# A third second-level product in the second block's second map, with weight sums and residual work placed elsewhere

## The chip, the cores and the metric

The kernel runs on one core of a Trainium2 chip. The metric is device time in microseconds (us) of one execution. A core has a matrix engine (TensorE, in profiles PE, with its weight loads PEld), three other engines that compute (VectorE or DVE, ScalarE or ACT, GpSimd or POOL) and a sync engine (SyncE or SP); each takes its instructions in order. SP issues most loads and POOL most stores. Data lie in SBUF, 128 partitions wide; TensorE's results go to eight PSUM banks.

## What is computed

One decoder layer over 2048 tokens of width 1024: a token mixer (convolution and pooling groups, one output projection), then a squared-ReLU MLP of hidden width 4096, each followed by a scaled residual and a layer norm. Cut to what matters here:

```python
h = x * (1.0 + sc2) + sh2
f = jnp.square(jax.nn.relu(h @ w_mlp_in[l])) @ w_mlp_out[l]
x = _layer_norm(DEEPNORM_ALPHA * x + (1.0 + g2) * f, ln2_g[l], ln2_b[l])
```

The first product of the MLP is called its first map below, the second its second map.

## The kernel before

The tokens go through in two blocks of 1024, b = 0 and b = 1, each through the input projection, the output projection, the first map (`up`, eight groups g) and the second map (`down`). Every product is made at higher precision from two halves: ScalarE rounds a tile to its high part (L81), VectorE makes the low part (L82), and `mm3` issues three matmuls (L86 to L88). A large product is done with seven block products instead of eight (Strassen's scheme), on sums of blocks that VectorE forms beforehand and that are stored to memory and loaded again where they are needed: `usum` for the MLP's inner activations, `w2sum` for its second weights.

In `down`, the block products are called coarse: product i is done in two steps (hf 0 and 1), each of 96 matmuls 128x512, into four banks X or Y. The results are combined into the eight tiles `F`. Where b = 1, two of the seven coarse products, i = 1 and i = 5, are done by the same scheme once more, over quarter blocks: seven `fine_*` products m of 48 matmuls 128x256 each (L1094 to L1148, the matmuls at L1120), on sums of quarter blocks of activations (`uquart`) and weights (`wquart`). `FINE` names the products with a fine form and where their operands lie; `save_quarters` makes the activations' sums in `up`, and `sum_blocks` the weights' from `in_w2q` (loads on SP, adds on VectorE, stores on POOL); `QUARTER_SUMS` says how many groups of the weights' sums follow each group g of block 1's first map. The first coarse result (i = 0, "11") is kept in `F`'s second half by `third_row` and added to other results by the rule of the scheme.

Tiles come from rings, named by a letter with a number of buffers: `h` 28, `r`, `w` 6, `o` 12. A tile that is asked for must wait until the tile that had its buffer before has been read for the last time. A scheduler orders each engine's instructions by its own estimate of times, so code that is written in one place can be issued earlier or later, and what decides is the order on each engine and the waits for buffers. The residual of the second layer norm (`residual()`, the tiles `rsave` made from `nsave` with two rows of the norm's parameters) is made beside `down`. The layer norm of the output projection ends in transposes on TensorE (L757).

## Time and profile before

| | |
|---|---|
| median of 3 runs | 1732.28 us (1731.45 to 1732.68) |
| profiled execution | 1732.22 us, its span 1730.2 us, granted clock 0.999 |
| TensorE | 7998 matmuls and transposes in the span |
| fine products (L1120) | 672 matmuls from 1467 to 1548 us |
| loads and stores | 480.48 MB, 278 GB/s on the mean |

The span is what lies between the first and the last instruction; the execution's time is 2 us longer. In block 0 the output projection ends at about 260 us, the first map at about 575, the second map at about 860; in block 1 the first map runs from about 1130 to 1420 and the second to the end. A timeline row has the start, the duration, the engine, the line, the operation with what it writes and reads, and in brackets the idle time ahead of it with what ended it. A windows row has the stretch, then PE, PEld, DVE, ACT and POOL busy in it with their instructions, the clock, the DMAs' busy share and GB/s.

### The profile page before, as it was taken

The numbers are of one execution on the slowest core, as the hardware profiler recorded it, in microseconds if no ns is written. First come the engines' busy times: TensorE is split into PE (matmuls) and PEld (weight loads), VectorE is DVE, ScalarE is ACT, GpSimd is POOL, SyncE is SP. The second block draws the span as 40 slices with busy tenths as digits, with TensorE's granted clock in tenths as the row PEclk, the third lists the DMA queues.
The fourth block names the chain that finished last, engine by engine and source line by source line (L and its number), as shares of the span: only waits on it lengthen the run. The fifth ranks groups of instructions, "written<-read, shape, count | busy, mean of one in ns | idle before, by whom it ended". The sixth has DMA issues, their size and how long they took to land.

```text
span 1730.2 us, 22371 instructions
## 1 busy us (share of the span) xinstructions
PE 1721.4 (99%) x7998; PEld 1440.3 (83%) x7998; DVE 1350.0 (78%) x1762; ACT 879.3 (51%) x1188; POOL 249.0 (14%) x449
## 2 busy tenths in 40 slices
PE   9999999999999999999999999999999999999998
PEld 8888888888888888888888888888888888998886
DVE  8898798877777676769686789688677768987796
ACT  5323358554454655446573344775445555773451
POOL 0222221122322000000000000103222222000020
PEclk9999999999999999999999999999999999999999
DMA  9899868778888998887672366557655589998871
GB/s 386 337 323 354 329 225 283 277 275 317 328 321 324 363 415 329 307 280 268 204 265 76 120 227 211 209 198 260 246 219 201 213 315 399 418 366 301 305 264 52
DMA packets 149647, 480.48 MB, mean 278 GB/s; under 512 B 17680, under 2 KB 18464, under 8 KB 149536
## 3 DMA queue, kind: packets, MB, share of 16 engines
q1 hardware_dynamic: 102528, 313.87, 50.0%
q0 software_dynamic: 47008, 165.19, 25.0%
q8 instruction: 62, 1.02, 0.2%
q14 instruction: 49, 0.40, 0.1%
HBM read 329.56 MB, written 149.43 MB: 277 GB/s over the span
## 4 chain that ended last, share of the span: by engine, by line
PE 99%; DVE 0%; ACT 0%; DVEq 0%; issue 0%
PE ps L87 30%; PE ps L88 30%; PE ps L86 30%; PE ps L1120 5%; PE ps L406 3%; PE ps L757 1%; PE ps L120 0%; PE ps L142 0%; DVE o L1354 0%; DVE o L1348 0%; DVE st L1321 0%; DVE o L91 0%; DVEq L1481 0%; ACT mv L721 0%; ACT mv L722 0%
## 5 line engine op out<-in xcount | busy, mean ns | idle before, releaser
L87 PE MATMUL ps<-h,w 128*128 128x512 f32 x1312 | 510.3, 389 | 0.0
L88 PE MATMUL ps<-h,w 128*128 128x512 f32 x1312 | 510.2, 389 | 0.0
L86 PE MATMUL ps<-h,w 128*128 128x512 f32 x1312 | 510.1, 389 | 0.0
L86 PE MATMUL ps<-h,h 128*128 128x512 f32 (+1 forms) x1000 | 387.7, 388 | 0.0
L88 PE MATMUL ps<-h,h 128*128 128x512 f32 (+1 forms) x1000 | 387.7, 388 | 0.0
L87 PE MATMUL ps<-h,h 128*128 128x512 f32 (+1 forms) x1000 | 387.5, 387 | 0.0
L81 ACT CAST h<-r 128x1024 fp32r<-128x1024 f32 (+1 forms) x196 | 199.2, 1020 | 280.3 <-PE ps L87 152.8
L81 ACT CAST w<-r 128x1024 fp32r<-128x1024 f32 x156 | 164.2, 1053 | 256.7 <-PE ps L87 247.2
L82 DVE TENSOR_TENSOR h<-r,h 128x1024 fp32r<-128x1024 f32 (+1 forms) x196 | 231.4, 1185 | 79.7 <-ACT h L81 79.3
L87 PEld LDWEIGHTS ps<-h,w 128*128 128x128 f32 x1312 | 246.3, 188 | 51.7 <-DVE h L82 0.5
L86 PEld LDWEIGHTS ps<-h,w 128*128 128x128 f32 x1312 | 246.0, 188 | 51.6 <-ACT h L81 0.3
L88 PEld LDWEIGHTS ps<-h,w 128*128 128x128 f32 x1312 | 246.3, 188 | 51.2 <-DVE w L82 0.3
L82 DVE TENSOR_TENSOR w<-r,w 128x1024 fp32r<-128x1024 f32 x156 | 190.5, 1221 | 98.3 <-ACT w L81 97.4
L86 PEld LDWEIGHTS ps<-h,h 128*128 128x128 f32 x1000 | 187.8, 188 | 38.4
L87 PEld LDWEIGHTS ps<-h,h 128*128 128x128 f32 x1000 | 187.8, 188 | 38.2
L88 PEld LDWEIGHTS ps<-h,h 128*128 128x128 f32 x1000 | 187.8, 188 | 38.2
L91 DVE TENSOR_TENSOR o<-o,o 128x1024 f32<-128x1024 f32 (+2 forms) x218 | 186.0, 859 | 43.0 <-DMA usum<-o 36.8
L82 DVE TENSOR_TENSOR h<-w,h 128x1024 fp32r<-128x1024 f32 x124 | 152.3, 1228 | 5.4 <-ACT h L81 5.4
L91 DVE TENSOR_TENSOR o<-o,ps 128x512 f32<-128x512 f32 (+1 forms) x172 | 112.4, 664 | 45.1 <-PE ps L88 44.7
L81 ACT CAST h<-w 128x1024 fp32r<-128x1024 f32 x124 | 130.2, 1050 | 14.8 <-POOL w L1059 4.3
L1003 POOL DMA_DIRECT2D usum<-o x96 | 51.5, 537 | 432.6 <-ACT o L997 199.8
L91 DVE TENSOR_TENSOR r<-r,r 128x1024 f32<-128x1024 f32 x60 | 73.4, 1223 | 14.2 <-DMA r<-in_w 8.7
(153 smaller groups left out, 1439.9 us busy)
## 6 DMA issues: line engine op xcount, KB each, us to landing
usum<-o POOLq DMA_DIRECT2D x96, 512.0 KB, 4.3
r<-usum SPq DMA_DIRECT2D x96, 512.0 KB, 5.2
w<-w2sum SPq DMA_DIRECT2D x64, 512.0 KB, 6.0
r<-in_w SPq DMA_DIRECT2D x60, 512.0 KB, 6.1
o<-in_w SPq DMA_DIRECT2D x72, 256.0 KB, 6.1
w2sum<-o POOLq DMA_DIRECT2D x64, 256.0 KB, 5.9
w<-in_w SPq DMA_DIRECT2D x32, 512.0 KB, 5.8
r<-uquart SPq DMA_DIRECT2D x28, 512.0 KB, 9.7
```

The source lines that it names most:

```text
L81: high = nc.scalar.copy(hi, src)
L82: return high.ins, nc.vector.tensor_tensor(lo, src, hi.bitcast(F32), op=ALU.subtract).ins
L86: nc.tensor.matmul(ps, whi, xhi, start=first, stop=False, skip_group_check=goes_on)
L87: nc.tensor.matmul(ps, whi, xlo, start=False, stop=False, skip_group_check=goes_on)
L88: nc.tensor.matmul(ps, wlo, xhi, start=False, stop=last, skip_group_check=goes_on)
L91: return nc.vector.tensor_tensor(out_, a, b_, op=op)
L406: nc.tensor.matmul(ps[m, h], wt[:, w : w + P], A[k][p // 2][:, hs], start=k == 0 and p == 0, stop=k == KD - 1 and p == 2)
L757: nc.tensor.transpose(ps[:, t * P : t * P + P], R[4 * h + t][:, k * P : k * P + P], ident)
L1003: nc.gpsimd.dma_start(usum[g, i], r)
L1120: nc.tensor.matmul(ps, a[:, us], w[:, gs], start=not begun, stop=hf == 1 and g == 3 and a is ul, skip_group_check=True)
```

## The change

Product i = 0 gets the fine form too: in block 1 the coarse list loses its two steps, and 21 fine products run in place of 14. Its result is made in `F[4..7]`'s first half and copied by ScalarE to the second; the results of k = 1 and k = 5 are then added from there by VectorE, eight adds of 128x512. The activations' quarter sums for it are made in `up` directly for g of 2 and more, and for g = 0 and 1 from a stored copy that is loaded again at g = 3 and 4.

The sums of quarter blocks of weights are twelve groups instead of eight: four are written in block 0's `down`, four in block 1's input projection and four in block 1's `up`. The first eight use a new ring `c` of two buffers, which result 11 of `up` also has, with the gate's vectors `G2` in block 0's `down`; ring `o` has 10 buffers instead of 12. The residual of block 1 is made in two parts: tiles 0 to 3 in `up` at g = 1, 3, 5 and 6 (two loads of rows and one of `nsave`, two VectorE operations, a store), tiles 4 to 7 in `down` by `rest_late`.

The order of the instructions changes well beyond these places. Three of them follow. First TensorE in block 1's first map, where `h_1519`, `h_1522` and their low parts `h_1520`, `h_1523` of before are the operands of one product, which is `h_1538` to `h_1542` after. Before:

```order
L86 MATMUL ps_1451_9094<-h_1519_9470,w_1526_9490 128x512
L86 MATMUL ps_1474_9218<-h_1503_9374,w_1532_9541 128x512
L87 MATMUL ps_1474_9218<-h_1504_9375,w_1532_9541 128x512
L88 MATMUL ps_1474_9218<-h_1503_9374,w_1533_9542 128x512
L86 MATMUL ps_1474_9218<-h_1503_9374,w_1532_9541 128x512
L87 MATMUL ps_1451_9094<-h_1520_9471,w_1526_9490 128x512
L88 MATMUL ps_1451_9094<-h_1519_9470,w_1527_9491 128x512
```

After:

```order
L89 MATMUL ps_1467_9206<-h_1538_9588,w_1545_9608 128x512
L90 MATMUL ps_1467_9206<-h_1539_9589,w_1545_9608 128x512
L89 MATMUL ps_1468_9219<-h_1538_9588,w_1545_9608 128x512
L90 MATMUL ps_1468_9219<-h_1539_9589,w_1545_9608 128x512
L91 MATMUL ps_1467_9206<-h_1538_9588,w_1546_9609 128x512
L89 MATMUL ps_1467_9206<-h_1538_9588,w_1545_9608 128x512
```

Before, matmuls of another product (bank `ps_1474`) stand between those of this one, which begins in its second bank only after six of its own in the first; after, the product runs without a break and goes to its second bank (`ps_1468`) with its third matmul.

On VectorE at the same place, the operations ahead of the low part of the product's last operand (`h_1523` before, `h_1542` after), with the low part of its weights `w_1527` before and `w_1546` after. Before:

```order
L91 TENSOR_TENSOR o_1518_9467<-o_1518_9467,o_1459_9160 128x1024
L91 TENSOR_TENSOR o_1510_9413<-o_1510_9413,ps_1501_9357 128x512
L91 TENSOR_TENSOR o_1502_9370<-o_1502_9370,ps_1451_9094 128x512
L82 TENSOR_TENSOR h_1520_9471<-o_1518_9467,h_1519_9470 128x1024
L91 TENSOR_TENSOR o_1502_9370<-o_1502_9370,ps_1452_9107 128x512
L91 TENSOR_TENSOR o_1521_9474<-o_1521_9474,o_1465_9186 128x1024
L82 TENSOR_TENSOR w_1537_9575<-r_1535_9572,w_1536_9574 128x1024
L82 TENSOR_TENSOR h_1523_9478<-o_1521_9474,h_1522_9477 128x1024
```

After:

```order
L94 TENSOR_TENSOR o_1537_9585<-o_1537_9585,o_1475_9272 128x1024
L94 TENSOR_TENSOR o_1529_9531<-o_1529_9531,ps_1520_9475 128x512
L94 TENSOR_TENSOR o_1521_9488<-o_1521_9488,ps_1467_9206 128x512
L85 TENSOR_TENSOR h_1539_9589<-o_1537_9585,h_1538_9588 128x1024
L94 TENSOR_TENSOR o_1540_9592<-o_1540_9592,o_1481_9298 128x1024
L94 TENSOR_TENSOR o_1521_9488<-o_1521_9488,ps_1468_9219 128x512
L85 TENSOR_TENSOR w_1546_9609<-r_1544_9606,w_1545_9608 128x1024
L85 TENSOR_TENSOR h_1542_9596<-o_1540_9592,h_1541_9595 128x1024
```

The add that empties the second bank (`ps_1452` before, `ps_1468` after) has moved behind a wide add, and the low part of this product's own weights has moved here from well ahead, while the next product's (`w_1537` before) has gone behind it.

On VectorE in block 0's second map, just ahead of the add that empties the first bank of a closing step (`ps_935` before, `ps_937` after). Before:

```order
L82 TENSOR_TENSOR h_1000_6354<-r_997_6349,h_999_6353 128x1024
L82 TENSOR_TENSOR h_1002_6358<-w_998_6351,h_1001_6357 128x1024
L82 TENSOR_TENSOR h_1006_6366<-r_1003_6361,h_1005_6365 128x1024
L82 TENSOR_TENSOR h_1008_6370<-w_1004_6363,h_1007_6369 128x1024
L91 TENSOR_TENSOR o_703_4831<-o_703_4831,ps_935_5925 128x512
```

After, from the third of these on:

```order
L85 TENSOR_TENSOR h_1010_6394<-r_1007_6389,h_1009_6393 128x1024
L85 TENSOR_TENSOR h_1012_6398<-w_1008_6391,h_1011_6397 128x1024
L94 TENSOR_TENSOR c_1259_7951<-c_1259_7951 128x512
L94 TENSOR_TENSOR c_1259_7951<-c_1259_7951,c_1260_7952 128x512
L94 TENSOR_TENSOR c_1260_7952<-c_1259_7951,c_1260_7952 128x512
L94 TENSOR_TENSOR c_1260_7952<-c_1260_7952 128x512
L94 TENSOR_TENSOR o_703_4831<-o_703_4831,ps_937_5939 128x512
```

Four adds of a group of quarter sums stand ahead of the bank's add, and four of another group (`c_1235`, `c_1236`) ahead of the two splits that are left out. On SP the loads of these groups stand among those of the residual and of the operands:

```order
L1082 DMA r_1013_6401<-usum_149 128x1024
L217 DMA w_1021_6444<-in_rows 128x1024
L954 DMA c_1235_7754<-in_w2q 128x512
L1227 DMA r_1019_6438<-rsave_152 128x1024
L217 DMA w_1022_6446<-in_rows 128x1024
L954 DMA c_1235_7754<-in_w2q 128x512
L954 DMA c_1236_7755<-in_w2q 128x512 x2
L1227 DMA r_1026_6487<-rsave_152 128x1024
L1084 DMA w_1042_6605<-w2sum_148 128x1024
L954 DMA c_1259_7951<-in_w2q 128x512
```

Before, the same stretch of SP has the rows without a `c` tile alone. The tile `c_1259` has the buffer that `c_1235` had.

The diff, cut to its core:

```diff
-QUARTER_SUMS = (0, 1, 1, 1, 1, 1, 1, 2)
+QUARTER_SUMS = (0, 0, 1, 0, 1, 1, 0, 1)
...
-        return mk(big, [P, w], dt, "o", 12)
+        return mk(big, [P, w], dt, "o", 10)
+
+    def t_c(w=T):
+        return mk(big, [P, w], F32, "c", 2)
...
             if not last:
+                quarter_sums(t_c)
                 next(groups[j])
+                quarter_sums(t_c)
...
-    FINE = {1: 0, 5: 1}
+    FINE = {0: 2, 1: 0, 5: 1}
+    QUARTERED = {1: 0, 7: 1, 0: 2}
+    REST = {1: 0, 3: 1, 5: 2, 6: 3}
...
+    def rest_of(t, r, ag, ab):
+        nc.vector.scalar_tensor_tensor(r, r, ALPHA, ag, op0=ALU.mult, op1=ALU.mult)
+        nc.vector.scalar_tensor_tensor(r, ab, ALPHA, r, op0=ALU.mult, op1=ALU.add)
+        nc.gpsimd.dma_start(rsave[t], r)
+
+    quarters = [(n, hf, p) for n in (2, 0, 1) for hf in range(2) for p in halves]
+
+    def quarter_sums(tiles):
+        n, hf, p = quarters.pop(0)
+        sum_blocks([w2q[n, i, hf] for i in range(4)], wquart[n, hf], tiles, [p])
...
         product(0, X, True)
-        c11 = keep(X)
+        c11 = keep(X, t_c)
         product(1, Y, True)
         join(c11, Y)
         save(c11, 0)
+        loaded = rest_loads()
...
+        if loaded:
+            rest_of(REST[g], *loaded)
         product(4, X, False)
...
-        coarse = (0, 2, 3, 4, 6) if b else (0, 1, 2, 3, 5, 4, 6)
+        coarse = (2, 3, 4, 6) if b else (0, 1, 2, 3, 5, 4, 6)
...
+            if b == 0 and n in (6, 8, 10, 12):
+                quarter_sums(lambda w: t_c(w))
...
-                    if m == 6:
-                        for t in range(4):
-                            add(t, lo_, X[t])
+                    if part_ < 6:
+                        continue
+                    for t in range(4):
+                        if k == 0:
+                            nc.scalar.copy(F[t + 4][:, hi_], F[t + 4][:, lo_])
+                            continue
+                        cs = lo_ if k == 1 else hi_
+                        tt(F[t][:, cs], F[t][:, cs], F[t + 4][:, lo_], ALU.add)
+                        if k == 5:
+                            add(t, hi_, X[t])
...
+            if b and g in (3, 4):
+                c11 = t_o()
+                nc.sync.dma_start(c11, usum[g - 3, 0])
+                save_quarters(c11, QUARTERED[0], g - 3)
+            for _ in range(QUARTER_SUMS[g] if b else 0):
+                quarter_sums(t_o)
```

More of the change, by code (lines that the diff above doesn't have):

```diff
@@ L1066, in down_operands, with rest_late @@
         return out_, done
+    def rest_late():
+        ag, ab = row(t_c(D), rows[0]), row(t_c(D), rows[1])
+        for t in range(4, 8):
+            yield
+            r = t_r()
+            nc.sync.dma_start(r, nsave[t])
+            rest_of(t, r, ag, ab)
     def residual():
@@ L1125, in quarter_of @@
             c = (H if i == 5 else 0) + col * Q
-            return [F[2 * row + t][:, c : c + Q] for t in range(2)]
+            return [F[(0 if i else 4) + 2 * row + t][:, c : c + Q] for t in range(2)]
         def fine_copy(i, row, col, bank):
@@ L1250, in down @@
         ready = operands(0)
-        later = residual()
+        later = rest_late() if b else residual()
         todo = [(k, m) for k in FINE for m in range(7)]
@@ L1402, in mlp @@
                     sums += [(sum_weights, wins[0], winsum, p) for p in halves]
-        else:
-            sums = [(sum_blocks, [w2q[n, i, hf] for i in range(4)], wquart[n, hf], p)
-                    for n in range(2) for hf in range(2) for p in halves]
         for g in range(NC):
@@ L1409, in mlp @@
                 pass
-            some = (QUARTER_SUMS if b else HALF_SUMS)[g]
-            for make, src, dst, p in sums[:some]:
+            if b and g in (3, 4):
[4 more added lines that the diff above has]
+                quarter_sums(t_o)
+            for make, src, dst, p in sums[:HALF_SUMS[g]]:
                 make(src, dst, t_o, which=[p])
-            del sums[:some]
+            del sums[:HALF_SUMS[g]]
         F = []
```

42 lines of the change are left out of this document (26 added, 16 removed).

## The prediction

> **What bounds the kernel now.** I read the page's busy shares first, then its chain of waits, because with five engines at 14 to 99% only the chain says which of them sets the end.
>
> ```profile
> PE 1721.4 (99%) x7998; PEld 1440.3 (83%) x7998; DVE 1350.0 (78%) x1762; ACT 879.3 (51%) x1188; POOL 249.0 (14%) x449
> ...
> PE 99%; DVE 0%; ACT 0%; DVEq 0%; issue 0%
> ```
>
> TensorE is busy for 1721.4 of 1730.2 us and is 99% of the chain; no other engine holds as much as 1%. There is nothing to win by waiting less: the 9 us left are the load at the head and the last tile's normalisation. So time falls only when TensorE's matmuls cost less, and it rises wherever an operand comes late. The change does a little of the first and moves a great deal of work that feeds TensorE, so the next views are the price of the two kinds of matmul and the stages in which feeding is tight.
>
> ```profile
> 1466.82 0.39 PE L87 MATMUL ps<-h,h 128*128 128x512 f32 x1
> 1467.05 0.39 PE L88 MATMUL ps<-h,h 128*128 128x512 f32 x1
> 1467.27 80.80 PE L1120 MATMUL ps<-h,h 128*128 128x256 f32 x672
> 1547.91 0.40 PE L86 MATMUL ps<-h,h 128*128 128x512 f32 x1
> ```
>
> This is TensorE's timeline around the stage of fine products. The rows of the wide matmuls are 0.39 us long, but they overlap: their starts are 0.227 us apart. The 672 narrow ones start at 1467.27 and the next wide one at 1547.91, so one costs 80.64 / 672 = 0.120 us.
>
> **Step 1, the matmuls.** Block 1 loses two coarse steps of 96 wide matmuls and gains seven fine products of 48 narrow ones. Removed: 192 x 0.227 = 43.5 us. Added: 336 x 0.120 = 40.3 us. Term: **-3.2 us**. That is 0.18% of the time and almost exactly what a measurement can tell from no change (0.2%, 3.5 us), so the side on which the kernel ends depends on the waits below.
>
> The Trainium skill, "TensorE: Matmul & The Clock Gate", section "Back-to-back issue gap", puts the isolated gap at N/2.4 + 2.5 ns, which is 109 ns for 256 columns and 216 ns for 512; by it the exchange would be 41.4 - 36.7, a gain of 4.7 us. The rows above speak against it, 0.120 and 0.227 here, and go before it.
>
> **Step 2, can VectorE and the DMAs feed 21 fine products in a row?** The windows view, with busy time and DMA share by stretch:
>
> ```profile
> 1467.00:1490.00 23.00, 23.00 (x192) 22.92 (x192) 21.63 (x21) 18.98 (x22) 0.00 (x0) 1.00 1.03 419
> 1490.00:1515.00 25.00, 25.00 (x210) 25.00 (x210) 23.21 (x25) 18.52 (x23) 0.00 (x0) 1.00 1.03 417
> 1515.00:1548.00 33.00, 33.00 (x277) 33.00 (x276) 29.58 (x30) 24.16 (x28) 0.00 (x0) 1.00 1.00 383
> ...
> L91 DVE TENSOR_TENSOR o<-o 128x512 f32<-128x512 f32 x6 | 4.1, 685 | 0.0
> ...
>   ACT h L81: 14.8, 22
> ```
>
> VectorE (the fourth figure) is busy for 21.63 + 23.21 + 29.58 = 74.4 of the 81 us, 5.3 us for each of 14 products that last 5.76. For 21 products that is 111.6 us, and the eight adds that bring the results home take 0.685 each by the next row (which shows such an add elsewhere), 5.5 us: 117 of 121 us. It fits, with 4 us to spare. Each product reads four operand pairs of 512 KB, 2.1 MB in 5.76 us or 364 GB/s, where the windows show up to 419. And the last row, of those who waited for line 1120, says that ScalarE waited 22 times for a fine matmul to give an operand buffer back, so the operands are made as far ahead as the ring allows, not just in time. Term: 0. The bounds: if nothing were ahead, VectorE's idle 6.2 us (81 - 74.4) would grow by half to 9.3 and the stage would need 126, 5 us more than TensorE takes; the other end is 0, and the ring puts it there.
>
> **Step 3, the quarter sums that now pass through two tiles of ring c.** Eight of the twelve groups are placed by the scheduler in block 0's second map, between 680 and 840 us. A group is four loads, four adds and four stores on the same two tiles, so a group's loads stand on SP until the stores of the group before have landed, and SP's operand loads and VectorE's operand splits queue behind them. Until 760 us this is hidden: the split at 739.79 ends at 741.0 and is first read by the matmul at 768.82, 28 us later. Then come three groups close together, just ahead of the stage that closes the block:
>
> ```profile
> 739.79 1.22 DVE L82 TENSOR_TENSOR h<-w,h 128x1024 fp32r<-128x1024 f32 x1
> ...
> 768.82 0.39 PE L87 MATMUL ps<-h,h 128*128 128x512 f32 x1
> ...
> 759.56 8.92 SPq L1055 DMA_DIRECT2D r<-usum  x2
> 768.57 0.38 SPq L214 DMA_DIRECT2D w<-in_rows  x1
> ...
> DMA to landing us min/median/max: 3.0/6.0/9.4
> ...
> o<-in_w SPq DMA_DIRECT2D x72, 256.0 KB, 6.1
> w2sum<-o POOLq DMA_DIRECT2D x64, 256.0 KB, 5.9
> ...
> 769.65 1.23 DVE L82 TENSOR_TENSOR h<-r,h 128x1024 fp32r<-128x1024 f32 x1 [3.08 <-ACT h L81]
> ...
> 779.67 0.69 DVE L91 TENSOR_TENSOR o<-o,ps 128x512 f32<-128x512 f32 x1 [2.23 <-PE ps L88]
> ...
> 784.00:821.00 37.00, 37.00 (x165) 30.65 (x164) 36.48 (x56) 25.65 (x47) 1.61 (x3) 1.00 0.74 251
> ...
> 813.04 1.22 DVE L82 TENSOR_TENSOR h<-w,h 128x1024 fp32r<-128x1024 f32 x1
> ...
> 821.86 0.39 PE L87 MATMUL ps<-h,h 128*128 128x512 f32 x1
> ```
>
> SP is free at 768.5 (its load before stood 8.9 us behind a store). With the page's landing times for loads and stores of 256 KB, the first group's loads land at 769 + 6.1, two adds (0.6 apart) let the first store go, and it lands 5.9 later: 782.2. The next group's loads land 6.1 later and its four adds end at 790.7. In VectorE's order these stand ahead of the add that started at 779.67: 11 us late. Three more sum adds follow, 1.8 us, and VectorE has no room to make it up, busy for 36.48 of the 37 us from 784 to 821. What covers it is the lead of the operand that is split at 813.04: ready at 814.26, first read at 821.86, 7.6 us. So by medians TensorE stands 11.0 + 1.8 - 7.6 = 5.2 us. The row of landing times is that of the residual's stores in this stretch: 3.0 at the least, 9.4 at the most. With 3.0 for all four transfers the lateness is 1.9 + 1.8, under the cover: 0. With one transfer of 9.4 among the four it is 8.6. I take **+3.0**, between the two cases and nearer the median one, because the stretch from 784 to 821 shows the DMAs busy only 0.74 of the time, which speaks for less than the medians of the whole page.
>
> The Trainium skill, "DMA: Bandwidth & Descriptors", section "Anatomy of one DMA", gives a transfer 2.0 us and its bytes at 436 GB/s, 2.6 us for 256 KB; by it the chain would stay under the cover and the term would be 0. That is the first rival below; the medians of this trace, 6.1 and 5.9, are against it.
>
> **Step 4, the start of block 1's first map.** Here the trace of before is tight. Two residual operations (1.28 us each by the first row, which shows one of the same form) and three more 512 KB loads are placed at 1137 to 1141 us, and the order of VectorE and TensorE changes behind them.
>
> ```profile
> 802.33 1.28 DVE L1354 SCALAR_TENSOR_TENSOR o<-o,mv,w 128x1024 f32<-128x1024 f32 x1
> ...
> 1158.08 1.22 DVE L82 TENSOR_TENSOR w<-r,w 128x1024 fp32r<-128x1024 f32 x1 [0.98 <-ACT w L81]
> ...
> 1163.29 0.68 DVE L91 TENSOR_TENSOR o<-o,ps 128x512 f32<-128x512 f32 x1
> 1163.89 1.22 DVE L91 TENSOR_TENSOR o<-o,o 128x1024 f32<-128x1024 f32 x1
> 1165.03 1.22 DVE L82 TENSOR_TENSOR w<-r,w 128x1024 fp32r<-128x1024 f32 x1
> 1166.89 1.23 DVE L82 TENSOR_TENSOR h<-o,h 128x1024 fp32r<-128x1024 f32 x1 [0.65 <-ACT h L81]
> ...
> 1162.45 0.63 PE L86 MATMUL ps<-h,w 128*128 128x512 f32 x2
> ```
>
> The product that begins at 1162.45 needs the split at 1166.89. Before, 12 matmuls of the next product filled the gaps; now all 12 come behind it. The lost time before this place is made up by the idle 0.98 and by operations moved back, so I put VectorE at the same time by 1160. The bank that the product's third matmul writes is emptied by the add at 1163.29, which ended at 1163.97 and now would at 1164.2. Before, TensorE had the fill until then; now it stands there from 1162.9 and waits 1.3. The split of the low half of this product's weights now comes right behind that add, 1164.2 to 1165.4, and the fifth matmul waits 0.7 more for it. Later operands, at 1164.8 and 1166.5, are in time. Less the 0.2 that was lost there before: **+1.8**. Bounds 0 (the rows shift by 2 us together) and 4 (both residual operations delay it in full).
>
> **Step 5, block 0's output projection.** Ring o falls from 12 to 10 and the last residual tiles load later.
>
> ```profile
> 254.75 2.11 PE L757 MATMUL ps<-ident,o 128*128 128x128 f32 x16
> 256.61 0.48 PE L86 MATMUL ps<-h,h 128*128 128x512 f32 x1
> ...
> 255.01 0.81 DVE L888 TENSOR_SCALAR o<-o,mv 128x1024 f32<-128x1024 f32 x1
> 255.73 0.69 DVE L91 TENSOR_TENSOR w<-w,w 128x512 f32<-128x512 f32 x1
> ```
>
> The transposes at 254.75 use the tile that VectorE finishes at 255.82. Two operations of 0.6 now stand ahead of that row, so it ends at 257.0; TensorE gets there at 255.8, and the matmuls that lay between the transposes come behind them. 1.2, less about 0.2 that was waited before: **+1.0**, between 0 (the shift is made up) and 3 (the load of the last tile is late as well). In block 0's first map the order shifts the same way as in step 4, but without the residual: 0, at most 1.
>
> The sum, against the profiled execution's 1732.2: -3.2 + 3.0 + 1.8 + 1.0 = +2.6, so 1734.8. The median of the runs, 1732.28, is the same within 0.1.
>
> **The rivals.** *Nothing waits.* Links take 3.0 us and the starts absorb the shifts: -3.2, 1729.0. For it, every wait above is a matter of 1 to 3 us, and TensorE lost next to nothing in a program with as many such joints; against it, the rows of steps 4 and 5 leave no lead to absorb a shift. *The c ring decides and it is slower.* Two links at the medians or above make step 3 cost 5 to 9 us; with 1.8 and 1.0 that is 1736.8 to 1740.8. It decides from a lateness of about 11.5 us at the add of 779.67, where step 3's wait reaches 3.9. For it, the medians; against it, the DMA share of 0.74, and that loads held back on SP leave the queues emptier for the rest. *The fine stage falls behind*, 5 us by step 2, 1734 alone, 1740 with the rest. *The change does not do what it says*: were a narrow matmul dearer among 1008 than among 672, by 0.01 us, the gain would be gone (336 x 0.13 = 43.7) and 1732.4 the time before any wait; against it, all 672 of them kept 0.120 on the mean.
>
> **How the numbers follow.** The forecast, part of the waits (1730.5 to 1735.7): 0.42. Nothing waits: 0.20, of which 0.06 lies over 0.2% below, as a few tenths less in step 1 put it there. The c ring: 0.26. The fine stage behind: 0.09. The narrow ones dearer: 0.03, on this side of the bound. Faster 0.06, slower 0.26 + 0.09 and 0.05 of the forecast's upper edge, 0.40, the rest same, 0.54. The range reaches from the first rival to the end of the second: 1728.8 to 1741.0.
>
> **What would show it.** Step 1: 1008 narrow matmuls at 0.120 and two coarse steps fewer. Step 2: VectorE near 97% in that stage and no gap of TensorE. Step 3: VectorE idle behind loads of the quarter weights at 770 to 790, and a gap of TensorE near 820; none there means that the first rival holds. Step 4: gaps of 1.3 and 0.7 near 1163. Step 5: one near 256. The forecast is wrong if TensorE loses more than 3 us at any place not named, above all among block 1's first map after 1200 or at the closing steps after 1590.

## The result and the profile after

| | before | after |
|---|---|---|
| median of 4 runs | 1732.14 us | 1775.84 us (1773.37 to 1780.13) |
| ratio, with its 95% interval | | 1.0255 (1.0233 to 1.0277) |
| profiled execution, its span | 1732.22, 1730.2 us | 1773.37, 1771.6 us |
| granted clock | 0.999 | 0.989 |
| loads and stores | 480.48 MB | 504.64 MB |

The change makes the kernel 2.55% slower, 43.7 us, where the prediction had +2.6 us and a range that ended at 1741.0. One slow run of the experiment on the rings alone (1907.76 us) is left out of its median below. These are the page's busy times and the head of its chain of waits, after:

```profile
PE 1734.4 (98%) x8142; PEld 1452.7 (82%) x8142; DVE 1391.9 (79%) x1840; ACT 888.8 (50%) x1206; POOL 272.0 (15%) x483
...
PE 65%; issue 13%; DMA 11%; DVE 8%; POOL 2%; ACT 1%; SPq 0%; DVEq 0%; POOLq 0%; ACTq 0%
```

TensorE still looks 98% busy, but it is no longer 99% of the chain: DMAs, VectorE and "issue" hold a third of it. A busy share hides this, because a matmul that runs at half clock counts as busy too (after some gaps TensorE runs at half clock for a few us, as the last section shows). So I measured lost time from TensorE's timeline of the whole span: where the start of the next matmul comes later than 0.2267 us (512 columns) or 0.120 us (256 columns) after a start, the excess is lost. Before, this gives 6.7 us, nearly all in the load at the head. After, it gives 51.3:

| place, after | us lost | of it at half clock |
|---|---|---|
| block 0's first map, at 316, and its end, 578 to 580 | 2.5 | |
| block 0's second map, 754 to 767 | 10.0 | 2.0 |
| block 0's second map, 824 to 847 | 13.2 | 4.0 |
| block 1's first map, 1172 to 1192 | 4.0 | |
| block 1's first map, 1371 to 1422 | 10.0 | 3.6 |
| fine products, 1518 to 1525 | 3.8 | 1.5 |
| closing steps, 1722 | 1.3 | |
| head and joints, as before | 6.5 | |

51.3 - 6.7 - 3.2 for the exchange of matmuls is 41.4, the difference of the two spans. So the whole result is a list of places. The largest are read here. In a row below, L81 is the rounding before the change and L84 after it, L82 and L85 VectorE's making of the low part, L91 and L94 its adds.

**The gap at 754.** First the rows of ScalarE before: two of the roundings of operands (L81), a copy that empties a bank of PSUM (L1181), and TensorE where it begins to write that bank again (the first row is the last matmul in the bank ahead of it).

```profile
741.36 1.05 ACT L81 CAST h<-r 128x1024 fp32r<-128x1024 f32 x1 [3.43 <-PE ps L87]
746.80 1.05 ACT L81 CAST h<-r 128x1024 fp32r<-128x1024 f32 x1 [3.44 <-PE ps L87]
...
748.70 0.58 ACT L1181 COPY o<-ps 128x512 f32<-128x512 f32 x1
...
752.04 0.39 PE L88 MATMUL ps<-h,h 128*128 128x512 f32 x1
752.27 0.39 PE L86 MATMUL ps<-h,h 128*128 128x512 f32 x1
```

The same after: four roundings (the last two are those of 741.36 and 746.80 before), the copy (now L1216), and TensorE.

```profile
737.56 1.06 ACT L84 CAST h<-r 128x1024 fp32r<-128x1024 f32 x1 [3.54 <-DMA r<-usum]
742.46 1.05 ACT L84 CAST h<-r 128x1024 fp32r<-128x1024 f32 x1 [2.90 <-DMA r<-usum]
750.96 1.05 ACT L84 CAST h<-r 128x1024 fp32r<-128x1024 f32 x1 [6.50 <-DVE r L94]
759.30 1.04 ACT L84 CAST h<-r 128x1024 fp32r<-128x1024 f32 x1 [6.34 <-DVE h L85]
...
761.20 1.55 ACT L1216 COPY o<-ps 128x512 f32<-128x512 f32 x3
...
754.13 0.39 PE L91 MATMUL ps<-h,h 128*128 128x512 f32 x1
761.83 0.79 PE L89 MATMUL ps<-h,h 128*128 128x512 f32 x1 [7.31 <-ACT o L1216]
...
787.45 0.39 PE L89 MATMUL ps<-h,h 128*128 128x512 f32 x1
```

Before, each rounding starts when TensorE gives a buffer back (the bracket names PE): the ring is full, and the operand is used some 28 us later, as step 3's rows show. After, the roundings start when a load or VectorE lets them, 5, 8 and 8 us apart where TensorE uses one every 5.44. Even the last of them, rounded by 760.3, is read by TensorE only at 787.45; TensorE didn't wait for it. It waited for the **copy behind the rounding**: ScalarE works in order, so the copy that frees the bank can't run before a rounding whose result nobody needs yet. Before, that copy ended at 749.28 and its bank was written at 752.27: the cover was 3.0 us, not 28. After, the first of the three copies ended at 761.78, 12.5 later; less 2.1 by which TensorE itself was late (754.13 + 0.23 instead of 752.27), less 3.0, that is 7.4, the gap.

Who made the roundings late is told by the waits of VectorE from 680 to 860 us (us in total, times, longest). Before:

```profile
DVE r L91 <- DMA r<-nsave: 17.4, 4, 6.9
DVE h L82 <- ACT h L81: 17.3, 7, 3.2
```

After, and below it two rows of SP's queue in the same stretch:

```profile
DVE c L94 <- DMA c<-in_w2q: 26.4, 8, 8.2
DVE r L94 <- DMA r<-nsave: 18.6, 4, 9.2
DVE h L85 <- ACT h L84: 3.4, 1, 3.4
...
SPq L1082 <- DVE h L85: 42.2, 14, 5.8
SPq L954 <- DMA wquart<-c: 37.6, 10, 8.5
```

The 17.3 us in which VectorE stood because the ring was full were the slack of this stage. In their place stand 26.4 us of waiting for quarter weights, 11.0 of them by 762 us, where the slack had been 9.9. The loads wait on SP (37.6 us) for the stores of the group before: with two tiles in ring `c`, each load stands behind the store that frees its tile.

**The gap from 824.** This is the place that step 3 named. After, VectorE's add that empties the first bank of the closing step (before at 779.67) and what stood ahead of it:

```profile
794.07 0.69 DVE L94 TENSOR_TENSOR c<-c 128x512 f32<-128x512 f32 x1 [8.23 <-DMA c<-in_w2q]
...
806.36 0.69 DVE L94 TENSOR_TENSOR c<-c 128x512 f32<-128x512 f32 x1 [4.88 <-DMA c<-in_w2q]
...
809.15 0.68 DVE L94 TENSOR_TENSOR o<-o,ps 128x512 f32<-128x512 f32 x1
...
825.96 0.51 PE L89 MATMUL ps<-h,h 128*128 128x512 f32 x1 [1.63 <-ACT h L84]
839.43 0.80 PE L90 MATMUL ps<-h,h 128*128 128x512 f32 x1 [3.64 <-DVE h L85]
```

The add is 29.5 us later than before, 17.4 after TensorE's own 12.1 (2.1 and the 10.0 of the gap at 754). Here the operands themselves run out, as the brackets of the last two rows show.

**Block 1's first map and the fine products.** TensorE and VectorE around 1413, then VectorE's waits from 1330 to 1422, then SP's from 1445 to 1530 and TensorE in the fine products:

```profile
1417.10 0.79 PE L89 MATMUL ps<-h,w 128*128 128x512 f32 x1 [3.60 <-DVE o L94]
...
1412.95 1.23 DVE L983 SCALAR_TENSOR_TENSOR o<-o,o 128x1024 f32<-128x1024 f32 x1 [10.46 <-DMA o<-nsave]
...
DVE o L983 <- DMA o<-nsave: 15.5, 2, 10.5
...
SPq L1135 <- DMA rsave<-r: 11.1, 1, 11.1
...
1520.45 5.82 PE L1155 MATMUL ps<-h,h 128*128 128x256 f32 x34 [2.09 <-ACT o L1165]
```

The residual's operations (L983) wait 10.5 us for their load of `nsave`; behind them in VectorE's order stand the adds that empty the banks. In the fine products a load of operands (L1135) waits 11.1 us for a tile of ring `r` that the residual holds until its store has landed.

### The profile page after: what moved, and what is told of

Its sections match the earlier page's. It is cut to its first block, busy times and chain, and to the rows that moved or that the text cites. A ratio compares the mean times of both kernels' runs of the same rounds, so it can differ in the third digit from the quotient of the medians.

```text
span 1771.6 us, 22926 instructions
## 1 busy us (share of the span) xinstructions
PE 1734.4 (98%) x8142; PEld 1452.7 (82%) x8142; DVE 1391.9 (79%) x1840; ACT 888.8 (50%) x1206; POOL 272.0 (15%) x483
## 2 busy tenths in 40 slices
DMA packets 157715, 504.64 MB, mean 285 GB/s; under 512 B 18832, under 2 KB 19616, under 8 KB 157600
## 4 chain that ended last, share of the span: by engine, by line
PE 65%; issue 13%; DMA 11%; DVE 8%; POOL 2%; ACT 1%; SPq 0%; DVEq 0%; POOLq 0%; ACTq 0%
PE ps L89 18%; PE ps L90 18%; PE ps L91 18%; PE ps L1155 6%; DVE o L94 3%; PE ps L409 2%; DVE h L85 2%; DMA usum<-c 2%; DMA o<-in_xT 2%; DMA r<-in_w 2%; DVE w L85 1%; DMA c<-in_wada 1%; DMA o<-in_w2q 1%; PE ps L762 1%; DMA r<-uquart 1%
## 5 line engine op out<-in xcount | busy, mean ns | idle before, releaser
L91 PE MATMUL ps<-h,w 128*128 128x512 f32 x1312 | 511.8, 390 | 0.4 <-DVE w L85 0.4
L89 PE MATMUL ps<-h,h 128*128 128x512 f32 (+1 forms) x936 | 365.8, 391 | 11.3 <-ACT o L1216 7.3
L90 PE MATMUL ps<-h,h 128*128 128x512 f32 (+1 forms) x936 | 365.9, 391 | 6.0 <-DVE h L85 6.0
L91 PE MATMUL ps<-h,h 128*128 128x512 f32 (+1 forms) x936 | 365.3, 390 | 0.0
L84 ACT CAST h<-r 128x1024 fp32r<-128x1024 f32 (+1 forms) x202 | 205.7, 1022 | 258.7 <-PE ps L90 68.2
L91 PEld LDWEIGHTS ps<-h,w 128*128 128x128 f32 x1312 | 247.3, 188 | 52.7 <-DVE w L85 0.8
L85 DVE TENSOR_TENSOR h<-r,h 128x1024 fp32r<-128x1024 f32 (+1 forms) x202 | 239.0, 1188 | 45.2 <-ACT h L84 44.6
L84 ACT CAST w<-r 128x1024 fp32r<-128x1024 f32 x156 | 164.3, 1054 | 208.8 <-PE ps L90 202.6
L85 DVE TENSOR_TENSOR w<-r,w 128x1024 fp32r<-128x1024 f32 x156 | 190.5, 1221 | 64.4 <-ACT w L84 63.3
L89 PEld LDWEIGHTS ps<-h,h 128*128 128x128 f32 x936 | 177.6, 190 | 49.9 <-ACT o L1216 7.7
L90 PEld LDWEIGHTS ps<-h,h 128*128 128x128 f32 x936 | 177.3, 189 | 43.5 <-DVE h L85 7.6
L91 PEld LDWEIGHTS ps<-h,h 128*128 128x128 f32 x936 | 177.5, 190 | 36.2
L85 DVE TENSOR_TENSOR h<-w,h 128x1024 fp32r<-128x1024 f32 x130 | 160.7, 1236 | 12.7 <-ACT h L84 12.5
L84 ACT CAST h<-w 128x1024 fp32r<-128x1024 f32 x130 | 136.6, 1051 | 9.3 <-DMA w<-in_w 3.4
L94 DVE TENSOR_TENSOR o<-o,o 128x512 f32<-128x512 f32 (+2 forms) x158 | 122.8, 782 | 5.5 <-DMA o<-hsave 2.4
L1155 PE MATMUL ps<-h,h 128*128 128x256 f32 x1008 | 122.9, 285 | 2.1 <-ACT o L1165 2.1
L1155 PEld LDWEIGHTS ps<-h,h 128*128 128x128 f32 x1008 | 122.6, 194 | 2.4 <-ACT o L1165 2.3
L94 DVE TENSOR_TENSOR o<-o,ps 128x512 f32<-128x512 f32 (+1 forms) x150 | 95.8, 650 | 27.8 <-PE ps L91 23.1
```

The source lines that it names most:

```text
L84: high = nc.scalar.copy(hi, src)
L85: return high.ins, nc.vector.tensor_tensor(lo, src, hi.bitcast(F32), op=ALU.subtract).ins
L89: nc.tensor.matmul(ps, whi, xhi, start=first, stop=False, skip_group_check=goes_on)
L90: nc.tensor.matmul(ps, whi, xlo, start=False, stop=False, skip_group_check=goes_on)
L91: nc.tensor.matmul(ps, wlo, xhi, start=False, stop=last, skip_group_check=goes_on)
L94: return nc.vector.tensor_tensor(out_, a, b_, op=op)
```

## The experiments

The first theory after the result: each part of the change that was moved (weight sums, residual, rings) makes an in-order engine wait, and the lost time lies where the part was put. Its rivals: the loads and stores are simply too many, or the third product itself can't be fed. The table behind the last experiment gives every kernel's lost time by stage, worked out as above.

**The rings alone.** The kernel before, with ring `o` at 10 and ring `c` of two tiles for result 11 and the gate's vectors:

```diff
-        return mk(big, [P, w], dt, "o", 12)
+        return mk(big, [P, w], dt, "o", 10)
...
-        c11 = keep(X)
+        c11 = keep(X, t_c)
```

> The kernel before with the rings of the change alone: o of 10, c of 2 for result 11 and for the gate's vectors in block 0's second map. Theory A (the rings by themselves do little; what costs is the work that is sent through them): the gaps of 2.0 near 578 and under 1 near 257 only, 1733 to 1736. Theory B (ring o of 10 makes the gaps of block 1's first map, which are there in every run with it but that with the residual put back): 1740 or more, with gaps between 1140 and 1420.

Measured: 1735.63 us (9 runs), ratio 1.0021 (1.0011 to 1.0031). It loses 2.1 us at 576 to 581, as the changed kernel does at 578, and 1.1 at 1166. So the rings by themselves cost 3 to 4 us. By the places, the gate's vectors pass through two tiles and result 11 leaves its tile late; this wasn't tested.

**The third product alone.** The sums of the third product are left out (it reads another product's), the early groups with them; the rings and the residual in block 1's second map are as before, first at the place where the kernel before puts it by count of steps:

```diff
-    FINE = {0: 2, 1: 0, 5: 1}
+    FINE = {0: 0, 1: 0, 5: 1}
...
-    REST = {1: 0, 3: 1, 5: 2, 6: 3}
+    REST = {}
...
-        base = 5
+        base = 2 if b else 5
...
-    quarters = [(n, hf, p) for n in (2, 0, 1) for hf in range(2) for p in halves]
+    quarters = [(n, hf, p) for n in (0, 1) for hf in range(2) for p in halves]
```

> The third fine product alone: it reads the quarter sums of another product, so its own sums are left out and the result is not the layer's; ring o has 12 buffers, there is no ring c, and the eight sums and the residual are where they were before. Both theories: 1729, the exchange of 192 wide for 336 narrow matmuls at 0.227 and 0.120 us. If the fine stage itself cannot be fed (the gaps of 3.8 us near 1520 and 1.3 near 1722 belong to it): 1732 to 1734.

Measured: 1746.86 us, ratio 1.0067 (1.0046 to 1.0089), where 1729 had been expected. No time is lost in the fine products, and 18.5 us at the closing steps from 1655: the residual's tiles are not ready for them.

The same with `base` 1 and 0 in block 1, so that the residual is made one and two steps earlier, among the fine products:

> The third fine product alone (own sums left out, result not the layer's), the residual one step later than in e6_third_base0: a quarter of it ahead of the fine stage instead of half, the rest behind it. If the transfers and VectorE work of the residual ahead of the fine stage make the gap of 7.6 us near 1485: it falls to 0 to 4, and the time to 1730 to 1736 unless the later tiles come late for the closing steps (gaps after 1640, as in e2_third_alone with one step more).

> The third fine product alone, again without its own sums (so the result is not the layer's), with old rings and old sums; the residual starts two steps earlier than in e2_third_alone, which keeps it three steps ahead of the step that reads it, as before. If the 18 us that e2_third_alone lost from 1655 to 1702 were the late residual: these gaps go, 1729 to 1731. If the third product makes VectorE late behind the fine stage whatever the residual does: gaps after 1550 stay, 1740 or more.

Measured: 1740.69 us, 1.0045 (1.0028 to 1.0062), and 1739.48 us, 1.0041 (1.0026 to 1.0056). Now 7.4 and 8.0 us are lost among the fine products, 4.9 and 0.7 at the closing steps. So the late residual did make the loss at the closing steps, but with `base` 1 I had expected 0 to 4 among the fine products. The wait of SP's queue there is that of the changed kernel, for `base` 1 and 0:

```profile
SPq L1133 <- DMA rsave<-r: 10.6, 1, 10.6
...
SPq L1133 <- DMA rsave<-r: 19.3, 3, 15.4
```

So the residual can be put wholly behind the fine products, its first four tiles in the steps right behind them:

```diff
-            if base <= n < base + 4:
+            for _ in range({2: 2, 3: 1, 4: 1}.get(n, 0) if b else base <= n < base + 4):
                 later.send(ready[1])
```

> The third fine product alone (own sums left out, result not the layer's), old rings, old sums, the residual wholly behind the fine stage, its first four tiles in the step right behind it. If the residual's tiles of ring r, held until their stores have landed, make the gap of 7.5 us near 1485: that gap goes, and less than the 12 to 18 us of e3_rest_back and e2_third_alone come late behind 1640: 0 to 6 us, 1729 to 1736. If the fine stage is too dense for 21 products by itself: a gap of 3 or more stays between 1467 and 1590.

Measured: 1735.60 us (10 runs), ratio 1.0020 (1.0011 to 1.0030). The page's group of the narrow matmuls (busy time, mean ns, idle time ahead), of this kernel and of the changed one:

```profile
L1153 PE MATMUL ps<-h,h 128*128 128x256 f32 x1008 | 121.1, 283 | 0.0
...
L1155 PE MATMUL ps<-h,h 128*128 128x256 f32 x1008 | 122.9, 285 | 2.1 <-ACT o L1165 2.1
```

The 21 fine products run without a gap, 121.1 / 1008 = 0.120 us a matmul. The 3.2 us that the exchange gains are more than used up at the closing steps, where the residual now is (4.0), and behind the last matmul (1.2). Even with its sums left out the product wins nothing at any of the four places of the residual.

**The residual back.** The changed kernel with the residual in block 1's second map (`REST` empty, `base` 2 as in the second experiment's diff), everything else kept.

> The changed kernel with block 1's residual made in the second map as before. Theory A: the gaps of 754 to 847 stay at 23 us, and of the 14 us lost in block 1's first map (1172, 1190, 1371, 1413) those at 1172 and 1190 go and the later two shrink, 1764 to 1770. Rival (ring o of 10 with the extra quarter stores makes them): the time stays within 3 of 1776.

Measured: 1769.24 us, ratio 1.0207 (1.0191 to 1.0222). The windows of the first map and of the fine products (the columns as for the kernel before; PE is the second figure), of the changed kernel and then of this one:

```profile
1130.00:1430.00 300.00, 291.55 (x1279) 239.21 (x1278) 226.51 (x297) 159.40 (x212) 66.94 (x110) 0.98 0.67 245
1460.00:1600.00 140.00, 137.91 (x953) 129.69 (x952) 117.92 (x122) 93.86 (x111) 9.00 (x15) 0.99 1.00 382
...
1130.00:1430.00 300.00, 299.99 (x1344) 248.88 (x1344) 229.56 (x307) 168.83 (x222) 70.01 (x114) 1.00 0.64 233
1460.00:1600.00 140.00, 140.00 (x1036) 134.20 (x1035) 118.22 (x118) 95.70 (x114) 4.37 (x8) 1.00 1.00 381
```

All that was lost in these two stages was the residual's, though the sums and result 11's ring are still there: 18 us. But the closing steps lose 11.2 us more and block 0's second map 2.1, so the time falls by 6.6 only.

**Fewer sums early.** The changed kernel with four groups early instead of eight, the rest in block 1's first map; then with none early (the same edit, and all twelve in the first map, on tiles of ring `o`):

```diff
-QUARTER_SUMS = (0, 0, 1, 0, 1, 1, 0, 1)
+QUARTER_SUMS = (0, 1, 1, 1, 1, 1, 1, 2)
...
-                quarter_sums(t_c)
                 next(groups[j])
-                quarter_sums(t_c)
```

> Only four groups of quarter sums stay in block 0's second map on ring c; the four of the input projection are written in block 1's first map on ring o, eight there as before. Theory A (a chain: each link adds its lag until the 28 us of lead are used up): four links of some 8 us use the lead but hardly pass it, the gaps of 754 to 847 fall to 0 to 8 us, 1752 to 1762. Rival (the volume of loads and stores counts, not the chain): half of 23 goes, about 1764.

```diff
-QUARTER_SUMS = (0, 0, 1, 0, 1, 1, 0, 1)
+QUARTER_SUMS = (1, 1, 1, 1, 2, 2, 2, 2)
...
-            if b == 0 and n in (6, 8, 10, 12):
-                quarter_sums(lambda w: t_c(w))
```

> The eight groups of quarter sums that stood in block 0's second map and in the input projection of block 1 are written in block 1's first map instead, all twelve on tiles of ring o; rings, residual and third product stay as changed. Theory A (the chain through the two tiles of ring c makes the gaps of 754 to 847 us, 23 us with the half-speed matmuls behind them): these gaps are gone, the time falls by 23 to about 1752, and by less if block 1's first map then waits more. Theory B (ring o of 10 and the residual's new places cost most of it, and would hold block 0 up all the same): the gaps of 754 to 847 stay, above 1765.

Measured: 1773.40 us, 1.0228 (1.0212 to 1.0243), and 1775.79 us, 1.0246 (1.0231 to 1.0261). The windows of block 0's second map from 760, of the changed kernel, of four groups early, and of none:

```profile
760.00:860.00 100.00, 90.71 (x364) 72.97 (x365) 76.47 (x107) 39.51 (x64) 11.37 (x21) 0.91 0.90 327
...
760.00:860.00 100.00, 97.49 (x420) 80.52 (x421) 79.49 (x107) 50.04 (x74) 2.67 (x5) 0.96 0.78 279
...
760.00:860.00 100.00, 100.00 (x443) 82.81 (x442) 74.69 (x102) 51.54 (x77) 2.15 (x4) 1.00 0.70 247
```

With four groups the gap at 754 stays (10.2 us) and the one from 824 is gone, with none both are: the first four make the one, the last four the other, and so these gaps are the groups'. Yet the time doesn't fall. The first map's loss grows from 14.5 to 20.7 and 33.0, the fine products' from 3.8 to 11.3 and 9.7. My theory had expected that most of the 23 us would be won; that was wrong. Groups that are moved bring their loads, adds and tiles along.

**What the chain of groups is bound by.** Three kernels with the early groups' parts on other engines: the adds on GpSimd; the loads issued by GpSimd; all of it on GpSimd.

```diff
-            tt(b22, b22, b12, ALU.subtract)
+            add(b22, b22, b12, ALU.subtract)
...
+    def pool_tt(out_, a, b_, op):
+        return nc.gpsimd.tensor_tensor(out_, a, b_, op=op)
```

> The changed kernel with the four adds of each of the eight early groups done by POOL instead of VectorE; loads on SP, stores and tiles as changed. If VectorE, standing in its fixed order before adds whose loads have not come, uses up the operands' lead: the gaps of 754 to 847 us fall from 23 to under 6, about 1753 to 1759. If SP's loads, standing behind the stores of the group before, do it: they stay at 15 or more, and grow if POOL is slower.

```diff
-                nc.sync.dma_start(r, src[i][:, p])
+                queue.dma_start(r, src[i][:, p])
...
+        sum_blocks([w2q[n, i, hf] for i in range(4)], wquart[n, hf], tiles, [p], nc.sync if tiles is t_o else nc.gpsimd)
```

> The changed kernel with the loads of the eight early groups of sums issued by POOL instead of SP, so that SP's operand loads stand behind none of them. If the operand loads held back on SP make the gaps of 754 to 847: they fall from 23 us to under 8, about 1755 to 1762. If VectorE, which takes its adds in order and waits in them for loads that wait for stores, makes them: 15 us or more stay, 1768 or more.

> The changed kernel with loads, adds and stores of the eight early groups all on POOL, so that neither SP nor VectorE stands behind the chain; tiles as changed. If the chain hurts through whichever in-order queue shares it (SP in e9_adds_pool, VectorE in e8_loads_pool): with both free the gaps of 680 to 850 us fall from 23 (after), 29 (e9) and 57 (e8) to under 10, the time to 1755 to 1765, with what POOL's own stores (the residual's) then wait for left over. If it is the traffic of 16 MB itself that takes the transfers' time: 15 or more stay.

Measured: 1782.15 us, 1.0287 (1.0268 to 1.0306); 1810.96 us, 1.0456 (1.0439 to 1.0474); 1815.08 us, 1.0482 (1.0463 to 1.0500). All are slower. For the last, the windows from 680, and three waits of its engines in that stretch:

```profile
680.00:760.00 80.00, 61.06 (x256) 49.44 (x255) 30.00 (x24) 21.85 (x25) 48.04 (x63) 0.87 0.81 293
760.00:860.00 100.00, 65.64 (x270) 53.35 (x269) 56.97 (x62) 29.93 (x41) 13.81 (x21) 0.83 0.78 279
...
DVE h L85 <- ACT h L84: 49.1, 4, 44.9
...
SPq L217 <- DMA xsum<-o: 29.5, 2, 29.0
SPq L1114 <- DMA rsave<-r: 26.1, 1, 26.1
```

I had thought that a chain taken off SP and VectorE would stop no one, and expected less than 10 us lost here; it was 61.6. GpSimd issues the other stores too, of the residual and of the input's sums (`xsum`). They now stood behind the chain, their tiles weren't freed, and SP's loads waited for these up to 29 us. The DMAs were busy 0.81 and 0.78 of the two stretches, less than the changed kernel's 0.93 and 0.90, at more lost time, so TensorE didn't stand because the DMAs were full. With the adds on GpSimd the chain is also longer: one takes 1.5 to 1.7 us there on the mean, against 0.69 on VectorE. What the waits of the three kernels show is that the chain passes its lateness to any in-order queue that it shares. That its two tiles set its pace is argued from SP's 37.6 us of waits for the stores of the group before; a ring of more tiles wasn't tried.

**Other places for all parts.** The whole third product with ring `o` at 12 and no ring `c`. First all twelve groups in block 1's first map and the residual in its second map, `base` 0:

> The whole third product with its sums, on the old rings (o of 12, no c): all twelve groups of weight sums in block 1's first map on ring o, the residual in the second map two steps earlier. Theory A (the early sums and the residual's new places are the cost): no gaps in block 0, few in block 1's first map, 1730 to 1738. Rival (twelve groups and a third product's stores are too much for block 1's first map wherever the residual is): 5 to 20 us of gaps from 1150 to 1470, 1738 to 1750.

Then four groups in block 1's input projection on tiles of ring `o`, eight in the first map, `base` 1; and the same with the residual behind the fine products:

```diff
-                quarter_sums(t_c)
+                quarter_sums(t_o)
                 next(groups[j])
...
-QUARTER_SUMS = (0, 0, 1, 0, 1, 1, 0, 1)
+QUARTER_SUMS = (0, 1, 1, 1, 1, 1, 1, 2)
```

> The whole third product with its sums: ring o of 12 and no ring c, four groups of sums in block 1's input projection on ring o (behind block 0's closing steps by the order of SP), eight in block 1's first map as before, the residual in the second map one step earlier than in e2_third_alone. Theory A (the place of the sums and of the residual costs, not their amount): no gaps from 750 to 850, under 6 in block 1's first map, 1732 to 1742. Rival (the third product's quarter stores and sums are too much for block 1's first map): 8 or more there, 1745 or more.

> The whole third product: ring o of 12, no ring c, four groups of sums in block 1's input projection, eight in its first map, the residual behind the fine stage as in e12_third_res_after. Theory A: the gaps of e11_in_o12_base1 near 1000 (5 us) and in the first map (4) stay, that of 7.4 near 1490 goes, 1736 to 1743; not faster than the kernel before.

Measured: 1761.19 us, 1.0167 (1.0152 to 1.0182); 1749.01 us, 1.0092 (1.0077 to 1.0107); 1744.91 us, 1.0071 (1.0055 to 1.0087). With twelve groups the first map loses 17.4 us, as the rival had it (5 to 20), so it can't hold them; the time lies above the rival's 1738 to 1750 too, because the fine products and the closing steps lose 14 more. With eight the first map loses 4.2, under the 6 that I had expected, but the projection now loses 5.1 and the time misses 1732 to 1742; the last kernel misses its 1736 to 1743 by 2. The best placement of the whole product that was tried, the last, loses 5.8 us in the input projection, 4.4 in the first map and 2.9 at the closing steps against a gain of 3.2.

Time lost by TensorE in us, by stage (the head, 5.5 to 6.4 us everywhere, left out):

| kernel | to 590 | block 0, second map | block 1, projections | first map | fine products | closing steps |
|---|---|---|---|---|---|---|
| before | 0.5 | 0.0 | 0.2 | 0.2 | 0.0 | 0.0 |
| **after** | 2.8 | 23.3 | 0.0 | 14.5 | 3.8 | 1.3 |
| rings alone | 3.1 | 0.0 | 0.5 | 1.3 | 0.0 | 0.0 |
| third alone, base 2 | 0.5 | 0.0 | 0.4 | 0.2 | 0.0 | 18.5 |
| third alone, base 1 | 0.9 | 0.0 | 0.2 | 0.2 | 7.4 | 4.9 |
| third alone, base 0 | 0.4 | 0.0 | 1.8 | 0.2 | 8.0 | 0.7 |
| third alone, residual behind | 0.6 | 0.0 | 0.7 | 0.2 | 0.0 | 4.0 |
| residual back | 1.9 | 25.4 | 0.0 | 0.1 | 0.0 | 12.5 |
| four groups early | 2.6 | 10.2 | 0.0 | 20.7 | 11.3 | 1.4 |
| no group early | 2.7 | 0.0 | 0.0 | 33.0 | 9.7 | 0.9 |
| twelve in first map, base 0 | 0.5 | 0.0 | 0.0 | 17.4 | 9.6 | 4.5 |
| four in projection, base 1 | 0.5 | 0.0 | 5.1 | 4.2 | 7.4 | 4.3 |
| the same, residual behind | 0.5 | 0.0 | 5.8 | 4.4 | 0.0 | 2.9 |
| adds on GpSimd | 2.4 | 29.4 | 0.9 | 16.4 | 4.1 | 1.2 |
| loads by GpSimd | 1.6 | 56.1 | 0.0 | 13.9 | 6.8 | 1.2 |
| all on GpSimd | 3.8 | 61.6 | 0.0 | 14.6 | 3.9 | 0.0 |

The first map's column separates its two causes. With four, eight and twelve groups in it the loss is 14.5, 20.7 and 33.0 with the residual there, and 0.1, 4.4 and 17.4 without: the residual costs 14 to 16 us whatever the sums do. (The rings differ: the kernels with 4.4 and 17.4 have `o` at 12 and no `c`.)

## Why the prediction was wrong, step by step

**Step 1, the matmuls, -3.2: right.** The narrow matmuls kept 0.120 us in the undisturbed stage, and the difference of the spans closes with 3.2. The rival that they get dearer fell.

**Step 2, the fine products, 0: right in its mechanism.** With the residual out of the way 21 products run without a gap (third alone, base 2 and residual behind; the residual put back). The 3.8 us that the changed kernel loses there are no shortage of VectorE but the tile of ring `r` that the residual's store holds.

**Step 3, the quarter sums, +3.0: this is the step that failed.** It cost 23.3 us, by three errors.
- "Until 760 us this is hidden: [...] 28 us later." The 28 us are the lead of an operand. But the operations that make it share their engines with the copies that empty the banks, whose cover was 3.0 us, and in an in-order engine the shortest cover behind a late operation counts. I had looked at when the late result is read, not at what stands behind the late operation. And the lead was taken as if each group found it whole. The lags add up: by 762 us VectorE had waited 11.0 us for quarter weights, beside the work of the adds themselves, and the slack up to there had been 9.9. This is the 10.0 us at 754, which the experiment with four groups early keeps and the one with none early loses.
- At the place that I did name, the chain was right: quarter weights first, the bank's add late, a gap near 820. The size was not. At the medians of the landing times I had the add 11.0 us late; it was 17.4. The links themselves were nearly as long as the medians say: from the first load to the bank's add the chain took 22.8 us (786.34 to 809.15), where the sum has 21.7 (769 to 790.7). What the sum left out is that the first group's loads stand in a queue as well. SP had waited 3.9 us behind a store of the residual and 1.6 behind one of the group before (its waits from 779.5 to 788 us), so the first load went at 786.34, which is 5.2 later than 769 when TensorE's own 12.1 are taken off. Less the cover of 7.6 the 17.4 leave 9.8; TensorE lost 13.2 from 824 to 847, of which 4.0 were half clock, a cost that the sum didn't have.
- Of the 5.2 us of gap that the medians gave I took 3.0, because the DMAs were busy 0.74 of that stretch. That share was the one before the change; from 760 to 860 it rose from 0.72 to 0.90. The Trainium skill's rule ("DMA: Bandwidth & Descriptors", section "Anatomy of one DMA — SWDGE (gpsimd) path", 2.6 us for 256 KB as an estimate) is given for transfers that GpSimd issues; here those are the groups' stores, while the loads are SP's. The trace agrees only in part: four stores issued from 777.3 landed after 6.0 to 8.4 us, four from 795.1 after 3.0 to 3.3. The four loads from 786.34 landed after 4.4 to 6.5, and the first add on them started at 794.07.

```profile
786.34 0.33 SPq L954 DMA_DIRECT2D c<-in_w2q  x1
```

**Step 4, the start of block 1's first map, +1.8: right in its mechanism, twice as large.** 4.0 at 1172 to 1192, the end of its bounds. It is the residual's operations: with the residual back it is gone. But the step asked only about the first of the four residual tiles. The ones at 1371 and 1413 cost another 10.0: there the residual's operations wait 5.1 and 10.5 us for a load of `nsave`, with the adds that empty the banks behind them. That sum was never made. The prediction itself called a loss in this map after 1200 what would make it wrong.

**Step 5, block 0's output projection, +1.0: wrong.** TensorE has no idle time from 254 to 262 us, before or after. The smaller ring showed elsewhere, at 578 (2.0 us, in the rings alone as well), where I had 0.

**The rivals.** "The c ring decides and it is slower" had the right side and the right mechanism, but priced one place at 9 us at the most, with the 28 us of lead taken for granted elsewhere. None of the rivals summed the residual's four tiles.

**Slips in the sums.** Step 3's chain has three transfers, not four, and its cases were worked out with three. The landing times of 3.0 to 9.4 us are those of eight stores and four loads of the residual, 512 KB each, where a group's transfers have 256 KB. The c ring decides from a lateness of 9.7 us at the add (11.5 with the three adds behind it), so the medians' own 11.0 already lay on that rival's side. And had a narrow matmul become dearer by 0.01 us, all 1008 would have been: 10.1 us, where the rival counts 336 of them, 3.4. The measured 0.120 leaves that rival nothing.

**What isn't settled.** A ring `c` of more tiles wasn't tried; it would tell whether the groups' chain can be broken. Why result 11 and the gate cost the rings alone 3 to 4 us was read from the places only. And the 4.0 us that the third product alone loses at the closing steps was not taken apart.

## What to carry to other kernels

An operand's lead isn't the cover of the operation that makes it: the cover is the shortest of what stands behind that operation on its in-order engine, above all a copy or an add that empties a PSUM bank. Lead is a stock that successive small delays use up together, so the lags of all groups are summed over a stage, and a chain of load, add and store on a ring of two tiles is late by the sum of its links in whichever queue it stands. Where every stage is fed just in time, moving work to another stage moves the gap with it: a gain of 3.2 us didn't pay for any of the places that were tried.

## What was unexpected of the hardware

After a gap TensorE's granted clock was half for some microseconds, and this made each gap dearer. The windows of the changed kernel (the figure before the last two is the clock): behind the gaps at 754 and 1413, behind the fine products' gap of 2.2 us, and behind one of 1.8 us at 1173.

```profile
762.00:767.00 5.00, 5.00 (x12) 3.92 (x13) 0.61 (x1) 3.23 (x5) 0.00 (x0) 0.51 1.00 383
1417.00:1422.20 5.20, 5.10 (x12) 4.04 (x13) 5.13 (x6) 2.09 (x3) 0.30 (x1) 0.50 0.24 101
...
1520.40:1524.60 4.20, 4.15 (x22) 4.15 (x23) 4.01 (x4) 3.84 (x4) 0.00 (x0) 0.60 1.02 417
...
1175.30:1180.00 4.70, 4.70 (x21) 3.85 (x22) 4.70 (x5) 2.26 (x4) 0.00 (x0) 1.00 0.08 19
```

At 0.51 the matmuls start 0.43 us apart, not 0.227. In the changed kernel half clock makes up 11 of the 51.3 us lost, and it lasted 3 to 5 us at a time. The length of a gap alone doesn't decide. In the changed kernel the gap of 1.8 us at 1173 was not followed by half clock, that of 2.1 at 1371 and all longer ones were. But a gap of 1.8 us at the same place was followed by it with four groups early (clock 0.60 from 1162.5 to 1165.5 us), with the adds on GpSimd (0.50 from 1182.2 to 1185.2) and with all on GpSimd (0.57 from 1215.4 to 1218.6). And one of 2.4 us at 1313, with no group early, was not (1.00 from 1315.4 to 1320). The Trainium skill, "TensorE: Matmul & The Clock Gate", section "Part 1: The HAM clock gate", knows the two clocks, full and half, and gives about 3.4 us of idle time for the fall; the half clock agrees, but here gaps of 1.8 us were enough in some kernels.
